# Token mixing in one-unit pieces, with new placement of weight scaling, transposes and the last outputs

## Chip, cores, metric

One core of one Trainium2 chip. The metric is device microseconds of one execution; medians of several runs are given.

## The reference, cut to what matters

```python
# x: (16, 2048, 256) float32; weights 256 x 256; time_mix vectors of 256
x_prev[:, 1:, :] = x[:, :-1, :]
xv = x * time_mix_v + x_prev * (1 - time_mix_v)
xr = x * time_mix_r + x_prev * (1 - time_mix_r)
v = xv @ value_weight
r = xr @ receptance_weight
out = (sigmoid(r) * v) @ output_weight      # the k branch is not used
```

## The kernel before

The 32,768 rows are worked in 64 units of 512 rows, four to a batch. In each unit TensorE transposes x (features on partitions), ScalarE copies the result from PSUM, the memory that TensorE writes to, into `xt` in SBUF, the engines' working memory, and the mix is `xt_prev * c + xt` with `c = 1/tm - 1`, after the weights have been multiplied by `tm`. The mix is one scale per half of the features (`ko`) and one add. Then come two projections (r, v), a sigmoid on ScalarE, the product z on VectorE, the output projection, and a copy and store.

The scale and add of a piece (`piece` is batch, r or v, and a range of columns). POOL, that is GpSimd, takes the second half of the features of some pieces:

```python
def scale(piece, kos=(0, 1)):                  # VectorE, 128 partitions x piece width
    for ko in kos:
        last = nc.vector.tensor_scalar(out=mix[b][:, m, ko, lo:hi], in0=xt[b][:, ko, lo:hi],
                                       scalar1=c_sb[:, m, ko:ko+1], op0=ALU.mult, ...)
    return last

def scale_pool(piece, after):                  # the same for ko = 1 on POOL ...
    op = nc.gpsimd.tensor_scalar(out=mix[b][:, m, 1, lo:hi], in0=xt[b][:, 1, lo:hi], ...)
    tc.add_manual_dep(op.ins, after.ins.name, SYNC, ...)   # ... not before `after` is done

def add(piece):                                # VectorE, both halves at once, both inputs in SBUF
    return nc.vector.tensor_tensor(out=mix[...], in0=mix[...], in1=xt[b][:, :, lo+P:hi+P], op=ALU.add)
```

The loop (cut). After the ramp, as the first eight or so passes are called here, each pass handles one piece of 1024 columns, `held`, and `last` is VectorE's scale of it:

```python
for g in range(NU - 1):
    project(ps_r, g, 0); sigmoid -> s_sb
    for i in todo:
        last = scale(pieces[i], (0,) if i in on_pool else (0, 1))
        if i not in held:
            last = add(pieces[i])
    advance(g + 7)                             # transposes seven units ahead
    project(ps_v, g, 1)
    z_sb = s_sb * ps_v                         # VectorE
    scale_pool(coming[-1], last)               # POOL's half of the next piece
    for i in held: add(pieces[i])
    wrap_slots()                               # once per batch: copy the shifted columns in xt
    output(g - 1, z_prev)
```

At the start two time-mix vectors are loaded with a 4-byte element as the innermost run, and POOL scales the weights.

## Time and profile before

| | before |
|---|---|
| median of the first three runs | 217.93 us (217.86 to 220.3) |
| span of the profiled execution | 217.6 us (this execution took 219.38 us) |
| TensorE / VectorE / ScalarE / POOL busy | 94 / 86 / 84 / 36% |
| first projection, z(0) | 13.39 us, 18.78 us |
| z start to start in the middle | 3.04 to 3.05 us |

A page of the profile gives spans counted from the first instruction; the time of an execution is some 1.8 us longer than its span (219.38 against 217.6). Groups of instructions by shape have these columns: line, engine, operation, output and inputs with their shapes, count, then busy us and mean ns of one, then the idle time of the engine before them and what ended it. Three groups of the kernel before:

```profile
L381 DVE TENSOR_TENSOR z_sb<-s_sb,psum_v 128x1024 bf16<-128x1024 bf16 x63 | 76.9, 1220 | 15.7 <-PE psum_v L235 13.9 <-ACT s_sb L370 1.5
L224 DVE TENSOR_TENSOR mix<-mix,xt 128x2048 bf16<-128x2048 bf16 x60 | 73.8, 1229 | 0.1
L211 POOL TENSOR_SCALAR mix<-xt,c_sb 128x1024 bf16<-128x1024 bf16 x58 | 64.7, 1115 | 107.6 <-DVE mix L200 82.0 <-PE psum_v L235 22.7 <-ACT xt L174 3.0
```

VectorE (DVE) waits 13.9 us in all for the v projection: it has time left. POOL is mostly released by a scale of VectorE (82.0 us of its waiting), and it works beside z in the middle of the run (start, length, what):

```profile
179.80 1.12 POOL L211 TENSOR_SCALAR mix<-xt,c_sb 128x1024 bf16<-128x1024 bf16 x1 [2.03 <-PE psum_v L235]
179.90 1.22 DVE L381 TENSOR_TENSOR z_sb<-s_sb,psum_v 128x1024 bf16<-128x1024 bf16 x1 [0.29 <-PE psum_v L235]
...
181.04 1.22 DVE L224 TENSOR_TENSOR mix<-mix,xt 128x2048 bf16<-128x2048 bf16 x1
```

### The profile page before, as it was taken

To read this page: it belongs to the slowest core of one execution; us is meant where nothing else is said; L and a number is where in the kernel's file an instruction comes from. 1 tells how busy PE (TensorE), PEld (TensorE's weight loads), DVE (VectorE), ACT (ScalarE), POOL (GpSimd) and SP (SyncE) were. 2 spreads that over 40 slices of the span, in tenths; PEclk is the share of its full clock that TensorE was granted. 3 is DMA by queue.
4 is the path that set the end of the run, shared out by engine and by line. 5 is a ranking of instruction groups with operands and counts; after the bars stand their busy time and mean duration, and the time that the engine had idled before them with its cause. 6 is when DMAs were issued, how large, how long until landed. Compare 5 with 4: busy or idle time off the path is not lost.

```text
span 217.6 us, 4124 instructions
## 1 busy us (share of the span) xinstructions
PE 204.7 (94%) x1590; PEld 135.9 (62%) x1590; DVE 186.1 (86%) x236; ACT 183.3 (84%) x196; POOL 78.8 (36%) x103
## 2 busy tenths in 40 slices
PE   8459989999999999999999999999999999999982
PEld 8336755666666666666666666666666666665561
DVE  0297999989898998989889998989998998999932
ACT  2227997999999999999999999999999999987781
POOL 3242423434452445434443345433453234433000
PEclk9957999999999999999999999999999999999999
DMA  5999899999999999999999998989999744335464
GB/s 138 296 219 215 172 164 346 199 270 279 248 286 188 360 166 351 200 289 245 247 285 202 342 172 352 199 295 239 264 270 211 304 194 196 146 143 209 200 270 194
DMA packets 9299, 52.03 MB, mean 239 GB/s; under 512 B 1472, under 2 KB 2368, under 8 KB 3520
## 3 DMA queue, kind: packets, MB, share of 16 engines
q0 software_dynamic: 2304, 16.25, 44.3%
q1 hardware_dynamic: 6144, 35.13, 39.6%
q10 hardware_dynamic: 832, 0.40, 0.6%
q8 instruction: 12, 0.20, 0.3%
q14 instruction: 7, 0.06, 0.1%
HBM read 34.47 MB, written 33.55 MB: 313 GB/s over the span
## 4 chain that ended last, share of the span: by engine, by line
PE 83%; DVE 7%; DMA 4%; issue 3%; ACT 1%; ACTq 0%; DVEq 0%
PE psum_v L235 24%; PE psum_o L245 24%; PE psum_r L235 23%; PE ps_t L169 11%; DMA tm_sb<-in_time_mix_v_dram 4%; DVE mix L224 3%; DVE mix L200 2%; DVE z_sb L381 1%; ACT o_sb L265 0%; DVE z_sb L285 0%; PE psum_v L245 0%; PE psum_r L245 0%; ACT o_sb L296 0%; ACTq L98 0%; ACTq L97 0%
## 5 line engine op out<-in xcount | busy, mean ns | idle before, releaser
L211 POOL TENSOR_SCALAR mix<-xt,c_sb 128x1024 bf16<-128x1024 bf16 (+1 forms) x60 | 66.1, 1101 | 112.8 <-DVE mix L200 84.9
L381 DVE TENSOR_TENSOR z_sb<-s_sb,psum_v 128x1024 bf16<-128x1024 bf16 x63 | 76.9, 1220 | 15.7 <-PE psum_v L235 13.9
L224 DVE TENSOR_TENSOR mix<-mix,xt 128x2048 bf16<-128x2048 bf16 (+2 forms) x69 | 79.9, 1158 | 0.3
L265 ACT COPY o_sb<-psum_o 128x1024 f32<-128x1024 f32 x63 | 64.0, 1016 | 16.0 <-PE psum_o L245 15.9
L235 PEld LDWEIGHTS <-w_bf 128*128 128x128 bf16 x520 | 48.8, 99 | 39.3 <-POOL w_bf L139 3.3
L370 ACT ACTIVATE s_sb<-psum_r 128x1024 bf16<-128x1024 f32 x63 | 65.2, 1034 | 5.4 <-PE psum_r L235 5.4
L235 PE MATMUL psum_r<-mix,w_bf 128*128 128x512 bf16 (+1 forms) x256 | 66.2, 381 | 3.1 <-DVE mix L224 3.1
L235 PE MATMUL psum_v<-mix,w_bf 128*128 128x512 bf16 (+1 forms) x256 | 66.2, 381 | 1.3 <-DVE mix L224 0.8
L245 PE MATMUL psum_o<-wo_bf,z_sb 128*128 128x256 bf16 x504 | 65.3, 273 | 0.2 <-ACT o_sb L265 0.2
L174 ACT COPY xt<-ps_t 128x1024 bf16<-128x1024 bf16 x62 | 63.0, 1030 | 0.0
L245 PEld LDWEIGHTS <-z_sb 128*128 128x128 bf16 x512 | 49.9, 98 | 20.3 <-DVE z_sb L285 1.0
L169 PEld LDWEIGHTS <-x_bf 128*128 128x128 bf16 x496 | 33.3, 100 | 13.8 <-issue 0.5
L169 PE MATMUL ps_t<-ident,x_bf 128*128 128x128 bf16 x496 | 37.9, 222 | 0.0
L200 DVE TENSOR_SCALAR mix<-xt,c_sb 128x1024 bf16<-128x1024 bf16 (+2 forms) x78 | 35.1, 460 | 0.1
L91 POOL DMA_DIRECT2D x_bf<-in_x_dram x16 | 9.3, 583 | 0.0
L128 DVE TENSOR_SCALAR tms<-tm_sb 128x4 f32<-128x4 f32 x1 | 0.2, 171 | 7.8 <-DMA tm_sb<-in_time_mix_v_dram 7.8
L119 PE MATMUL psum_o<-zeros 128*128 128x128 bf16 x34 | 3.8, 313 | 1.0 <-DVE zeros L79 1.0
L119 PEld LDWEIGHTS <-zeros 128*128 128x128 bf16 x34 | 3.5, 150 | 1.0 <-DVE zeros L79 1.0
L174 ACT CAST xt<-psum_o 128x1024 bf16<-128x1024 f32 x1 | 1.0, 1012 | 3.6 <-PE psum_o L169 3.6
L169 PE MATMUL psum_o<-ident_f,x_unit 128*128 128x128 f32 x8 | 1.1, 276 | 2.7 <-DMA x_unit<-in_x_dram 2.7
L139 POOL TENSOR_SCALAR w_bf<-w_f,tms 128x256 bf16<-128x256 f32 x4 | 2.0, 518 | 4.2 <-DVE tms L131 4.1
L322 DVE COPY xt<-xt 128x254 bf16<-128x254 bf16 x15 | 3.3, 220 | 0.0
(38 smaller groups left out, 19.0 us busy)
## 6 DMA issues: line engine op xcount, KB each, us to landing
out_dram<-o_sb SPq DMA_DIRECT2D x30, 1024.0 KB, 5.6
x_bf<-in_x_dram POOLq DMA_DIRECT2D x15, 1024.0 KB, 11.1
out_dram<-o_sb SPq DMA_DIRECT2D x3, 512.0 KB, 2.6
x_unit<-in_x_dram SPq DMA_DIRECT2D x2, 256.0 KB, 3.8
x_unit<-in_x_dram SPq DMA_DIRECT2D x1, 512.0 KB, 7.0
x_bf<-in_x_dram POOLq DMA_DIRECT2D x1, 512.0 KB, 8.5
w_f<-n_receptance_weight_dram SPq DMA_DIRECT2D x1, 256.0 KB, 5.1
w_f<-in_value_weight_dram SPq DMA_DIRECT2D x1, 256.0 KB, 7.2
```

Source lines behind the costliest of these rows:

```text
L91: nc.gpsimd.dma_start(out=x_bf[b][:, lo:hi, :], in_=rows(b)[:, lo:hi, :])
L119: nc.tensor.matmul(out=warm[:, 0, 0:P], lhsT=zeros, rhs=zeros, start=True, stop=True)
L169: nc.tensor.transpose(out=ps[:, ko, jj * P : (jj + 1) * P], in_=src[:, jj, ko * P : (ko + 1) * P], identity=idn,)
L174: nc.scalar.copy(out=xt[b][:, :, c0 : c0 + TU], in_=ps)
L200: last = nc.vector.tensor_scalar(out=mix[b][:, m, ko, lo:hi], in0=xt[b][:, ko, lo:hi], scalar1=c_sb[:, m, ko : ko + 1], scalar2=None, op0= ...
L211: op = nc.gpsimd.tensor_scalar(out=mix[b][:, m, 1, lo:hi], in0=xt[b][:, 1, lo:hi], scalar1=c_sb[:, m, 1:2], scalar2=1.0, op0=ALU.mult, op1 ...
L224: return nc.vector.tensor_tensor(out=mix[b][:, m, :, lo:hi], in0=mix[b][:, m, :, lo:hi], in1=xt[b][:, :, lo + P : hi + P], op=ALU.add,)
L235: nc.tensor.matmul(out=ps[:, mo, :], lhsT=w_bf[:, m, ko, mo * P : (mo + 1) * P], rhs=mix[b][:, m, ko, e * TU + lo : e * TU + hi], start=(k ...
L245: nc.tensor.matmul(out=ps[:, slot, :], lhsT=z[:, ko, jj * P : (jj + 1) * P], rhs=wo_bf[:, ko, :], start=(ko == 0), stop=(ko == KO - 1),)
L265: nc.scalar.copy(out=o_sb[b][:, j0 : j0 + UJ, :], in_=ps)
L370: nc.scalar.activation(out=s_sb, in_=ps_r, func=ACT.Sigmoid)
L381: nc.vector.tensor_tensor(out=z_sb, in0=s_sb, in1=ps_v, op=ALU.mult)
```

## The change

The intent is an earlier start and less work ahead of need. Mixing goes in pieces of one unit (512 columns) shortly before use, transposes run four units ahead, the time-mix vectors come as contiguous rows and are turned by TensorE, the weights are scaled by ScalarE and VectorE (the output weights are cast by their load), ScalarE takes a few scales in the first loop and the last ones, some loads of x are gated behind the first, and the last two outputs go by halves. The core of the diff, with cuts marked:

```diff
-    LOOK = 7
+    LOOK = 4
+    AHEAD = 8
...
+    for m, tm in enumerate([time_mix_r, time_mix_v]):        # contiguous rows, then one transpose
+        nc.scalar.dma_start(out=tm_rows[m*KO:(m+1)*KO, :], in_=tm.rearrange("(ko p) -> ko p", p=P))
     nc.scalar.dma_start(out=x_last, in_=rows(0)[:, J - 1, :])
-    nc.scalar.dma_start(out=tm_sb[:, 0, :], in_=time_mix_r.rearrange("(ko p) -> p ko", p=P))
-    nc.scalar.dma_start(out=tm_sb[:, 1, :], in_=time_mix_v.rearrange("(ko p) -> p ko", p=P))
...
-            nc.gpsimd.tensor_scalar(out=w_bf[:, m, ko, :], in0=w_f32[:, m, ko, :], ...)
+        nc.scalar.activation(out=w_bf[:, 0, ko, :], in_=w_f32[:, 0, ko, :], func=ACT.Copy, scale=...)
...
+        nc.vector.tensor_scalar(out=w_bf[:, 1, ko, :], in0=w_f32[:, 1, ko, :], ...)
...
     for g in range(NU - 1):
+        lead = 2 * g + (4 if g < AHEAD else 5)
+        todo = [pieces(k // 2)[k % 2] for k in range(done, min(lead, 2 * NU))]
+        held = todo[-1:] if lead <= 2 * NU else []
...
+            by_pool = [p for p in pieces(g + 2) if p not in todo or p in held]
...
+        for p in todo:
+            if p[0] in late_copies:
+                wrap_slots()
+            if g > 0:
+                scale(p, [ko for ko in range(KO) if (p, ko) not in elsewhere])
+        for p in todo:
+            if p not in held:
+                last = add(p)
         ps_v = ...; project(ps_v, g, 1)
         z_sb = ...
+        for p in by_pool:
+            scale_pool(p, last)
+        for p in held:
+            add(p)
-        wrap_slots()
```

POOL now has two scales of 512 columns per unit; `last` is now an add, not a scale; and the wrap copy now stands between two scales of VectorE.

More of the change, by code (lines that the diff above doesn't have):

```diff
@@ L47 @@
     NU = B * UB
-    HALF = J * P // 2
-    LOOK = 7
-    SMALL = 2
+    LOOK = 4
     H = UJ // 2
-    START_T = [3, 5, 7, 9]
-    START_MIX = [4, 6, 8, 10, 12]
+    START_T = [1, 3, 5, 6, 7]
+    AHEAD = 8
     WARM = 34
-    WARM2 = 10
+    WARM2 = 12
     consts = ctx.enter_context(tc.tile_pool(name="consts", bufs=1))
@@ L94 @@
     x_unit = consts.tile([P, 2, UJ, D], FP32)
-    tm_sb = consts.tile([P, 2, KO], FP32)
-    w_f32 = consts.tile([P, 3, KO, D], FP32)
+    tm_rows = consts.tile([2 * KO, P], FP32)
+    w_f32 = consts.tile([P, 2, KO, D], FP32)
+    for m, tm in enumerate([time_mix_r, time_mix_v]):
+        nc.scalar.dma_start(
+            out=tm_rows[m * KO : (m + 1) * KO, :], in_=tm.rearrange("(ko p) -> ko p", p=P)
+        )
     nc.scalar.dma_start(out=x_last, in_=rows(0)[:, J - 1, :])
-    nc.scalar.dma_start(out=tm_sb[:, 0, :], in_=time_mix_r.rearrange("(ko p) -> p ko", p=P))
-    nc.scalar.dma_start(out=tm_sb[:, 1, :], in_=time_mix_v.rearrange("(ko p) -> p ko", p=P))
     for h in range(2):
@@ L108, with warm_up @@
     nc.sync.dma_start(out=w_f32[:, 1], in_=value_weight.rearrange("(ko p) n -> p ko n", p=P))
-    nc.sync.dma_start(out=w_f32[:, 2], in_=output_weight.rearrange("(ko p) n -> p ko n", p=P))
     sig0 = consts.tile([P, 1], BF16)
     nc.scalar.activation(out=sig0, in_=zeros[:, 0:1], func=ACT.Sigmoid)
+    w_bf = consts.tile([P, 2, KO, D], BF16)
+    wo_bf = consts.tile([P, KO, D], BF16)
     gate = consts.tile([P, 1], FP32)
     nc.gpsimd.tensor_copy(out=gate, in_=x_last[:, 0:1])
-    load(0, 2 * UJ, J)
-    load(1)
-    warm = ps_o_pool.tile([P, UJ, D], FP32, name="psum_o")
-    for _ in range(WARM):
-        nc.tensor.matmul(out=warm[:, 0, 0:P], lhsT=zeros, rhs=zeros, start=True, stop=True)
+    load(0, 2 * UJ, 3 * UJ)
+    nc.gpsimd.dma_start(out=wo_bf, in_=output_weight.rearrange("(ko p) n -> p ko n", p=P))
+    load(0, 3 * UJ, J)
+    nc.gpsimd.tensor_copy(out=gate, in_=x_unit[:, 1, 0, 0:1])
+    load(1, 3 * UJ, J)
+    load(1, 0, UJ)
+    load(1, UJ, 3 * UJ)
+    load(2)
+    def warm_up(n):
+        ps = ps_t_pool.tile([P, P], FP32, name="ps_t")
+        for _ in range(n):
+            nc.tensor.matmul(out=ps, lhsT=zeros, rhs=zeros, start=True, stop=True)
+    warm_up(WARM)
     def new_xt(b):
@@ L127, with coefficients @@
     c_sb = consts.tile([P, 2, KO], FP32)
-    nc.vector.tensor_scalar(
-        out=tms, in0=tm_sb, scalar1=0.0, scalar2=1e-30, op0=ALU.is_equal, op1=ALU.mult
-    )
-    nc.vector.tensor_tensor(out=tms, in0=tms, in1=tm_sb, op=ALU.add)
-    nc.vector.reciprocal(c_sb, tms)
-    nc.vector.tensor_scalar(out=c_sb, in0=c_sb, scalar1=-1.0, scalar2=None, op0=ALU.add)
-    w_bf = consts.tile([P, 2, KO, D], BF16)
-    wo_bf = consts.tile([P, KO, D], BF16)
-    for m in range(2):
-        for ko in range(KO):
-            nc.gpsimd.tensor_scalar(
-                out=w_bf[:, m, ko, :],
-                in0=w_f32[:, m, ko, :],
-                scalar1=tms[:, m, ko : ko + 1],
-                scalar2=1.0,
-                op0=ALU.mult,
-                op1=ALU.mult,
-            )
-        if m == 0:
-            load(2)
-    nc.gpsimd.tensor_scalar(
-        out=wo_bf, in0=w_f32[:, 2], scalar1=1.0, scalar2=1.0, op0=ALU.mult, op1=ALU.mult
-    )
+    def coefficients():
+        ps = ps_o_pool.tile([P, 2, KO], FP32, name="psum_o")
+        nc.tensor.transpose(
+            out=ps.rearrange("p m k -> p (m k)"), in_=tm_rows, identity=ident_f[: 2 * KO, : 2 * KO]
+        )
+        tm = consts.tile([P, 2, KO], FP32)
+        nc.vector.tensor_copy(out=tm, in_=ps)
+        nc.vector.tensor_scalar(
+            out=tms, in0=tm, scalar1=0.0, scalar2=1e-30, op0=ALU.is_equal, op1=ALU.mult
+        )
+        nc.vector.tensor_tensor(out=tms, in0=tms, in1=tm, op=ALU.add)
+        nc.vector.reciprocal(c_sb, tms)
+        nc.vector.tensor_scalar(out=c_sb, in0=c_sb, scalar1=-1.0, scalar2=None, op0=ALU.add)
+    coefficients()
     def transposes(i):
@@ L178, in first_transposes, with half @@
     def first_transposes():
-        pl = ps_t_pool.tile([P, KO, P], FP32, name="ps_t")
-        for ko in range(KO):
-            nc.tensor.transpose(
-                out=pl[:, ko, 0:P], in_=x_last[:, ko * P : (ko + 1) * P], identity=ident_f
-            )
-        nc.vector.tensor_copy(out=xt[0][:, :, 1:P], in_=pl[:, :, 0 : P - 1])
-        for h, (pool, name) in enumerate([(ps_r_pool, "psum_r"), (ps_v_pool, "psum_v")]):
+        def half(h, pool, name):
             ps = pool.tile([P, KO, TU], FP32, name=name)
@@ L195, in first_transposes @@
             nc.scalar.copy(out=xt[0][:, :, c0 : c0 + H * P], in_=ps[:, :, 0 : H * P])
+        half(0, ps_r_pool, "psum_r")
+        pl = ps_t_pool.tile([P, KO, P], FP32, name="ps_t")
+        for ko in range(KO):
+            nc.tensor.transpose(
+                out=pl[:, ko, 0:P], in_=x_last[:, ko * P : (ko + 1) * P], identity=ident_f
+            )
+        nc.vector.tensor_copy(out=xt[0][:, :, 1:P], in_=pl[:, :, 0 : P - 1])
+        half(1, ps_v_pool, "psum_v")
     def scale(piece, kos=(0, 1)):
@@ L199, in scale @@
         for ko in kos:
-            last = nc.vector.tensor_scalar(
+            nc.vector.tensor_scalar(
                 out=mix[b][:, m, ko, lo:hi],
@@ L206, in scale @@
             )
-        return last
     def scale_pool(piece, after):
@@ L218, in scale_pool @@
         )
-        if after is not None:
-            tc.add_manual_dep(op.ins, after.ins.name, SYNC, reason="one at a time")
+        tc.add_manual_dep(op.ins, after.ins.name, SYNC, reason="one at a time")
     def add(piece):
@@ L281, in last_unit @@
             nc.scalar.activation(out=s_sb[:, :, lo:hi], in_=banks[h], func=ACT.Sigmoid)
-        output(g - 1, z_prev)
         for h, (lo, hi) in enumerate(cols):
@@ L287, in last_unit, with tile_for, pieces, ready @@
             )
-        for h, (pool, name) in enumerate([spare[0], spare[2]]):
+        spare = [(ps_o_pool, "psum_o"), (ps_r_pool, "psum_r"), (ps_v_pool, "psum_v"), (ps_t_pool, "ps_t")]
+        for k, (pool, name) in enumerate(spare):
             ps = pool.tile([P, H, D], FP32, name=name)
+            h = k % 2
             for jj in range(H):
-                out_matmuls(ps, z_sb, h * H + jj, jj)
-            lo = e * UJ + h * H
+                out_matmuls(ps, z_prev if k < 2 else z_sb, h * H + jj, jj)
+            lo = (e - 1) * UJ + k * H
             if h == 0:
+                nc.scalar.copy(out=o_sb[b][:, lo : lo + H, :], in_=ps)
+            else:
                 nc.vector.tensor_copy(out=o_sb[b][:, lo : lo + H, :], in_=ps)
-            else:
-                nc.scalar.copy(out=o_sb[b][:, lo : lo + H, :], in_=ps)
-            store((nc.sync, nc.scalar)[h], b, lo, lo + H)
-    pieces = []
-    for b in range(B):
-        for q in range(2):
-            step = TU if 2 * b + q < SMALL else HALF
-            for lo in range(q * HALF, (q + 1) * HALF, step):
-                pieces += [(b, m, lo, lo + step) for m in range(2)]
-    def needs(piece):
-        b, m, lo, hi = piece
-        if b == 0:
-            return hi // TU
-        return UB * b + min(hi // TU, UB - 1) + 1
-    def tile_for(piece):
-        if piece[0] not in mix:
-            mix[piece[0]] = mixpool.tile([P, 2, KO, J * P], BF16, name="mix")
+            store(nc.scalar if k == 3 else nc.sync, b, lo, lo + H)
+    def tile_for(b):
+        if b not in mix:
+            mix[b] = mixpool.tile([P, 2, KO, J * P], BF16, name="mix")
+    def pieces(g):
+        b, e = divmod(g, UB)
+        tile_for(b)
+        return [(b, m, e * TU, (e + 1) * TU) for m in range(2)]
+    def ready(g):
+        b, e = divmod(g, UB)
+        return tnext > (g if b == 0 else UB * b + min(e + 1, UB - 1))
     def wrap_slots():
@@ L337 @@
     first_transposes()
-    tile_for(pieces[0])
+    tile_for(0)
     for h in range(2):
@@ L342, with scale_act @@
         add(half)
-    scale(pieces[1])
-    add(pieces[1])
-    for _ in range(WARM2):
-        nc.tensor.matmul(out=warm[:, 0, 0:P], lhsT=zeros, rhs=zeros, start=True, stop=True)
-    advance(1)
-    done = 2
-    on_pool = set()
-    def plan(g):
-        upto = START_MIX[g] if g < len(START_MIX) else g + 4 + 2 * SMALL
-        upto = min(upto, len(pieces))
-        for i in range(upto, len(pieces)):
-            assert UB * pieces[i][0] + pieces[i][2] // TU > g + 1, (g, i)
-        return list(range(done, upto))
-    z_prev = None
-    todo = plan(0)
+    for ko in range(KO):
+        nc.scalar.activation(
+            out=w_bf[:, 0, ko, :], in_=w_f32[:, 0, ko, :], func=ACT.Copy, scale=tms[:, 0, ko : ko + 1]
+        )
+    scale(pieces(0)[1])
+    add(pieces(0)[1])
+    for ko in range(KO):
+        nc.vector.tensor_scalar(
+            out=w_bf[:, 1, ko, :],
+            in0=w_f32[:, 1, ko, :],
+            scalar1=tms[:, 1, ko : ko + 1],
+            scalar2=None,
+            op0=ALU.mult,
+        )
+    warm_up(WARM2)
+    advance(1)
+    scale(pieces(1)[0])
+    add(pieces(1)[0])
+    z_prev = None
+    elsewhere = set()
+    done = 3
+    def scale_act(piece, kos):
+        b, m, lo, hi = piece
+        for ko in kos:
+            nc.scalar.activation(
+                out=mix[b][:, m, ko, lo:hi],
+                in_=xt[b][:, ko, lo:hi],
+                func=ACT.Copy,
+                scale=c_sb[:, m, ko : ko + 1],
+            )
+            elsewhere.add((piece, ko))
     for g in range(NU - 1):
-        for i in todo:
-            assert needs(pieces[i]) <= tnext, (g, i, tnext)
-            tile_for(pieces[i])
-        done += len(todo)
+        lead = 2 * g + (4 if g < AHEAD else 5)
+        todo = [pieces(k // 2)[k % 2] for k in range(done, min(lead, 2 * NU))]
+        held = todo[-1:] if lead <= 2 * NU else []
+        done = lead
         ps_r = ps_r_pool.tile([P, KO, TU], FP32, name="psum_r")
@@ L370 @@
         nc.scalar.activation(out=s_sb, in_=ps_r, func=ACT.Sigmoid)
-        last = None
-        held = todo[-1:] if g > 0 else []
-        for i in todo:
-            last = scale(pieces[i], (0,) if i in on_pool else (0, 1))
-            if i not in held:
-                last = add(pieces[i])
-        advance(START_T[g] if g < len(START_T) else g + LOOK)
+        advance(START_T[g] if g < len(START_T) else g + LOOK)
+        if g + LOOK >= NU and g + 2 < NU:
+            scale_act(pieces(g + 2)[1], (0,))
+        by_pool = []
+        if 0 < g < NU - 2 and ready(g + 2):
+            by_pool = [p for p in pieces(g + 2) if p not in todo or p in held]
+        elsewhere.update((p, 1) for p in by_pool)
+        for p in todo:
[6 more added lines that the diff above has]
+                last = add(p)
         ps_v = ps_v_pool.tile([P, KO, TU], FP32, name="psum_v")
         project(ps_v, g, 1)
+        if g == 0:
+            scale_act(todo[0], (0, 1))
+            advance(2)
         z_sb = zpool.tile([P, KO, TU], BF16, name="z_sb")
         nc.vector.tensor_tensor(out=z_sb, in0=s_sb, in1=ps_v, op=ALU.mult)
-        coming = plan(g + 1)
-        for i in coming[-1:]:
-            if needs(pieces[i]) <= tnext:
-                if pieces[i][0] in late_copies:
-                    wrap_slots()
-                tile_for(pieces[i])
-                scale_pool(pieces[i], last)
-                on_pool.add(i)
-        for i in held:
-            add(pieces[i])
-        wrap_slots()
+        for p in by_pool:
+            if p[0] in late_copies:
+                wrap_slots()
+            scale_pool(p, last)
+        for p in held:
+            add(p)
         if z_prev is not None:
@@ L395 @@
         z_prev = z_sb
-        todo = coming
     last_unit(NU - 1)
```

## The prediction

> **What bounds the kernel now.** I read the busy shares first, then the chain that ended last, then the timeline of VectorE (DVE) and GpSimd (POOL). The page's busy line, and the chain: start, length in us, what.
>
> ```profile
> PE 204.7 (94%) x1590; PEld 135.9 (62%) x1590; DVE 186.1 (86%) x236; ACT 183.3 (84%) x196; POOL 78.8 (36%) x103
> ```
>
> ```profile
> 1.66 7.66 DMA tm_sb<-in_time_mix_v_dram
> ...
> 13.39 1.87 PE psum_r L235 x4
> 15.26 1.71 PE ps_t L169 x16
> 16.96 1.72 PE psum_v L235 x4
> ...
> 57.93 0.87 PE psum_o L245 x8
> 60.97 0.87 PE psum_o L245 x8
> ```
>
> TensorE is busy 94%, and in the middle the chain's output groups recur every 3.04 to 3.05 us (57.93 to 60.97). That is its own work for a unit of 512 rows: in the timeline r, v and output take 0.87 each, the eight transposes 0.45, together 3.05. 64 units at 3.05 are 195 us of the 217.6 us span. The rest is the start (first projection at 13.39, held up by two time-mix loads of 1 KB each, the second 7.66 us under way), a ramp to about 37 us, and the end. The first three groups take twice their later time (1.87, 1.71, 1.72 against 0.86, 0.90, 0.86), about 2.7 us lost.
>
> How near the next engine is, the timeline of VectorE shows (start, length, what, in brackets the idle time before):
>
> ```profile
> 176.85 1.22 DVE L381 TENSOR_TENSOR z_sb<-s_sb,psum_v 128x1024 bf16<-128x1024 bf16 x1 [0.29 <-PE psum_v L235]
> 177.99 1.22 DVE L224 TENSOR_TENSOR mix<-mix,xt 128x2048 bf16<-128x2048 bf16 x1
> 179.13 0.48 DVE L200 TENSOR_SCALAR mix<-xt,c_sb 128x1024 bf16<-128x1024 bf16 x1
> 179.90 1.22 DVE L381 TENSOR_TENSOR z_sb<-s_sb,psum_v 128x1024 bf16<-128x1024 bf16 x1 [0.29 <-PE psum_v L235]
> ```
>
> From start to start z takes 1.14 and the add 1.14; the scale ends at 179.61; the idle time is 0.29 us of 3.05. The waits between 37 and 192 us add up to 12.2 us on VectorE in 46 units, 0.27 each. A change that gives VectorE more than this per unit makes it the bound.
>
> The start of the timeline has the two sizes that the change uses, and a collision (POOL is busy from 25.33 to 26.45):
>
> ```profile
> 23.30 0.61 DVE L200 TENSOR_SCALAR mix<-xt,c_sb 128x512 bf16<-128x512 bf16 x2
> 23.94 0.69 DVE L224 TENSOR_TENSOR mix<-mix,xt 128x1024 bf16<-128x1024 bf16 x1
> 25.33 1.12 POOL L211 TENSOR_SCALAR mix<-xt,c_sb 128x1024 bf16<-128x1024 bf16 x1 [2.95 <-ACT xt L174]
> 26.05 0.94 DVE L224 TENSOR_TENSOR mix<-mix,xt 128x1024 bf16<-128x1024 bf16 x1
> ```
>
> The same add takes 0.69 us alone and 0.94 when it starts beside a POOL scale: it ends as if it had begun at 26.30, 0.15 before POOL's recorded end. Four larger adds of the ramp (at 30.48, 35.44, 38.22, 41.04) give 0.14 to 0.15 too.
>
> **What the Trainium skill says.** "SBUF — State Buffer", Who interferes with whom: a VectorE instruction with two SBUF inputs contends with a GpSimd instruction that reads SBUF; whichever starts first has the shared pair for the whole instruction. The trace agrees (0.94 against 0.69). z reads one operand from PSUM, so it should not be held; it took 1.22 beside POOL as elsewhere. "VectorE: DVE Perf Modes", The TRN2 errata: a fixed cost per instruction. It agrees: a scale of 512 columns takes 0.35, of 1024 0.48, so halving pieces nearly doubles the fixed part. "DMA: Bandwidth & Descriptors", Rules for kernel authors: a non-contiguous last dim lowers to one descriptor per element. The slow time-mix loads (4.9 and 7.7 us for 1 KB, against 3.6 us for 128 KB of x) fit. "TensorE: Matmul & The Clock Gate", Part 1: TensorE runs at half rate after an idle window; the doubled groups after an idle wait until 13.39 agree.
>
> **The change, part by part.**
>
> *Time-mix as rows.* Two loads of contiguous rows, one transpose of four columns on TensorE, one copy. Estimate: rows landed by 4.3; the warm-up matmuls end at 4.6 to 4.8; transpose and copy to 5.3; the four small VectorE operations take from 9.42 to 10.39 today, so coefficients at 6.3 in place of 10.39.
>
> *Weights on ScalarE and VectorE, output weights cast by the load, later x loads gated.* POOL is out of the path. The first weights land at 6.75 (1.65+5.1); ScalarE needs about 0.45 each, so they are ready near 8. Half pieces of unit 0: 6.75 to about 8.5. TensorE's order still has the transposes of unit 1 ahead of the first projection; their x landed at 9.1 beside POOL's x loads, which are now smaller or gated, so I take 8.0 plus 1.06. First projection near 9.1: **4.3 us earlier**, after a shorter idle time, so perhaps at full clock.
>
> *Start on VectorE.* From 8.5: the v piece (two scales and add, 1.25) to 9.7; two weight scales to 10.3; the r piece of unit 1, 1.25, to 11.6; z(0) at 11.6 (18.78 today). Then z 1.13 and a held add 0.61 to 13.35, four scales 1.04 and an add 0.61, z(1) at 15.0 (21.43 today). So far 6.4 us gained.
>
> *Steady state: pieces of one unit.* By the instruction order of the built program, VectorE has in each unit scale, scale, add, z, add (adds of 128x1024, scales of 128x512), and POOL two scales of 128x512 where it had one of 128x1024. Start-to-start times from the ramp: scale 0.26 (0.61 for two, the last 0.35), add 0.61, z 1.13. Sum 2x0.26+2x0.61+1.13 = 2.87. The wrap copy, every fourth unit, now stands between two scales and the second waits for it: 0.25 each time, 0.06 per unit. Without collisions 2.93, under 3.05.
>
> But POOL's pair starts only after the first add has completed, and the second add follows z, so they meet. Let the first add start at a. It ends at a+0.69; POOL starts 0.09 to 0.20 later (the gaps in the trace), I take 0.14; POOL's 128x512 scale takes 0.69 (17.54 and 21.70), the next 0.63 after the first; the port is free 0.15 before the recorded end: a+0.69+0.14+0.63+0.69-0.15 = a+2.00. Without POOL the second add would start at a+0.61+1.13 = a+1.74. So it is held 0.26. The loop closes at a+2.00+0.61+0.26+0.26 = a+3.13, with the wrap **3.19 us per unit**, against TensorE's 3.05: VectorE becomes the bound, by 0.14. Lookahead does not help against an engine that lacks time.
>
> *Transposes four ahead.* No work is removed: TensorE's 3.05 per unit stays. Today's last seven loops have no transposes and run at 2.6 to 2.75; now only three do.
>
> *The end.* z(62) started at 208.15 and the span ended 9.45 later. With the last two outputs by halves: z(62) ends 1.2 after its start, v by halves 1.0, then output halves and copies pipelined on both engines, and 3.6 from the last copy to the end as now; I get 8.6, gain 0.8.
>
> *Sum.* z(61) = 15.0+60x3.19 = 206.4; z(62) after a shorter loop (ScalarE and POOL have done its scales) +2.3 = 208.7; +8.6 = 217.3 span, against 217.6. The gain of the start is eaten at 0.14 per unit.
>
> **Rivals.**
> *TensorE stays the bound.* If POOL's pair is some 0.15 us quicker, or an add gets in between, the loop is 3.05. From 9.1, all later TensorE work is 64x2.61+62x0.45 = 195; plus about 1.5 of ramp stalls and 4 from the last matmul to the end: near 209.5. For it: 2.93 without collision fits under 3.05, and someone who moved work so carefully probably looked for this. Against: five adds show the hold.
> *Something between*: a loop of 3.10 to 3.15 gives 212 to 215.
> *Input limits the start.* The x loads by POOL take 8.5 to 11 us; if unit 2's piece is late, up to 2 us of the early gain are lost, hidden wholly or partly if TensorE alone is the bound, added if VectorE is.
> *The clock.* If the first groups again run at half rate, 2.7 us come back on TensorE, but VectorE's chain would hide most of them.
>
> **Range and chances.** The sum says 217.3; each 0.01 in the loop is 0.6 us, and my loop is good to 0.05, so 3 us; TensorE as bound gives 209.5. Six to four between the two, with the ground between filled: 215. Faster by 2% means under 213.6, a loop under 3.13: 0.38. Slower by 2% is over 222.3, a loop over 3.27: 0.04.
>
> **What would show it.** Coefficients near 6.3 and first projection near 9 show the start right. In the middle: z start to start 3.19, TensorE idle about 0.14 per unit waiting for VectorE, VectorE with no idle time and one of its two adds lengthened from 0.69 to about 0.95, show the collision. z start to start 3.05 with VectorE still waiting for psum_v, both adds near 0.69, or POOL done before the second add starts, would show it wrong. A late x_bf in the waits before 17 us would show the input rival.

## The result, and the profile after

The changed kernel takes 226.71 us (226.43 to 226.96, four runs) against 217.94 for the kernel before. The ratio is 1.0375, 95% interval 1.0305 to 1.0445. Ratios here are the mean time of one kernel's fast runs over that of the other's fast runs of the same rounds, so not quite the ratio of the medians. The prediction's estimate was 215, the sum of its working 217.3.

The busy line of the page, and the engines of the chain that ended last:

```profile
PE 211.0 (94%) x1593; PEld 136.4 (61%) x1593; DVE 211.8 (94%) x354; ACT 186.5 (83%) x202; POOL 96.0 (43%) x165
```

```profile
DVE 79%; issue 6%; PE 6%; DMA 3%; POOL 1%; SPq 1%; DVEq 0%; ACT 0%; POOLq 0%
```

TensorE still reads 94% busy, and it is no longer the bound: 79% of the chain is VectorE's. A busy share of 94% for both engines would not have told this; the chain does.

The start went as planned. From the timeline (start, length, what):

```profile
5.84 0.17 DVE L152 TENSOR_SCALAR c_sb<-c_sb 128x4 f32<-128x4 f32 x1
...
9.72 1.03 PE L239 MATMUL psum_r<-mix,w_bf 128*128 128x512 bf16 x4
...
12.23 1.21 DVE L412 TENSOR_TENSOR z_sb<-s_sb,psum_v 128x1024 bf16<-128x1024 bf16 x1
```

Coefficients end at 6.01 us, the first projection starts at 9.72 in place of 13.39 at the pace of the later ones (1.03 for four matmuls, as in the middle), and z(0) at 12.23 in place of 18.78. The clock that the trace shows as granted to TensorE is 1.00 from 9.7 to 15.0 us; before, it was 0.51 from 13.3 to 18.7.

One loop in the middle, the timeline with TensorE's and ScalarE's lines left out:

```profile
102.12 0.68 DVE L228 TENSOR_TENSOR mix<-mix,xt 128x1024 bf16<-128x1024 bf16 x1
...
102.72 1.21 DVE L412 TENSOR_TENSOR z_sb<-s_sb,psum_v 128x1024 bf16<-128x1024 bf16 x1
...
102.97 1.36 POOL L216 TENSOR_SCALAR mix<-xt,c_sb 128x512 bf16<-128x512 bf16 x2 [1.83 <-DVE mix L228]
...
103.86 1.00 DVE L228 TENSOR_TENSOR mix<-mix,xt 128x1024 bf16<-128x1024 bf16 x1
...
104.78 0.60 DVE L206 TENSOR_SCALAR mix<-xt,c_sb 128x512 bf16<-128x512 bf16 x2
...
105.31 0.68 DVE L228 TENSOR_TENSOR mix<-mix,xt 128x1024 bf16<-128x1024 bf16 x1
```

The first add starts at 102.12, the next first add at 105.31: 3.19 us. No idle time stands in brackets on VectorE. The loss is hidden in a length: the second add takes 1.00 where the first takes 0.68. It ends as if it had begun at 104.18, which is 0.15 before the recorded end of POOL's pair (104.33). From z(8) to z(61) z's starts are 3.19 apart in three loops of four and 3.46 in the fourth: 3.26 on average, against 3.05 in a regular loop before. In the fourth the wrap copy stands between two scales, which then start 0.58 apart in place of 0.26:

```profile
111.11 0.34 DVE L206 TENSOR_SCALAR mix<-xt,c_sb 128x512 bf16<-128x512 bf16 x1
111.37 0.21 DVE L324 COPY xt<-xt 128x254 bf16<-128x254 bf16 x1
111.69 0.35 DVE L206 TENSOR_SCALAR mix<-xt,c_sb 128x512 bf16<-128x512 bf16 x1
```

TensorE shows it from its side, with a wait for z that adds up to 4.6 us in 17 waits (before, one of 0.5):

```profile
100.80 1.02 PE L239 MATMUL psum_v<-mix,w_bf 128*128 128x512 bf16 x4 [0.26 <-DVE z_sb L412]
```

In the ramp a second collision appears at two batch boundaries. The wrap copy releases POOL just as VectorE's own scales come:

```profile
20.62 1.64 POOL L216 TENSOR_SCALAR mix<-xt,c_sb 128x512 bf16<-128x512 bf16 x2 [2.74 <-DVE xt L324]
...
20.93 1.48 DVE L206 TENSOR_SCALAR mix<-xt,c_sb 128x512 bf16<-128x512 bf16 x2
```

Two scales that take 0.60 elsewhere take 1.48, and z(2) to z(3) takes 3.88; so does z(6) to z(7). The instructions lengthened here read one tensor each, not two.

Where the 7.3 us between the two spans came from, by the starts of z: z(1) is 5.8 us earlier (15.67 against 21.43); the 60 loops from z(1) to z(61) take 197.7 us against 184.0, 13.7 more; the last loop and the end are 0.6 shorter.

### The profile page after: what moved, and what is told of

It reads as the page before. It is cut to its first block, busy times and chain, and to the rows that moved or that the text cites. A ratio compares the mean times of both kernels' runs of the same rounds, so it can differ in the third digit from the quotient of the medians.

```text
span 224.9 us, 4329 instructions
## 1 busy us (share of the span) xinstructions
PE 211.0 (94%) x1593; PEld 136.4 (61%) x1593; DVE 211.8 (94%) x354; ACT 186.5 (83%) x202; POOL 96.0 (43%) x165
## 4 chain that ended last, share of the span: by engine, by line
DVE 79%; issue 6%; PE 6%; DMA 3%; POOL 1%; SPq 1%; DVEq 0%; ACT 0%; POOLq 0%
DVE mix L228 40%; DVE z_sb L412 29%; DVE mix L206 9%; DMA x_unit<-in_x_dram 3%; PE psum_v L239 2%; POOL mix L216 1%; PE psum_o L249 1%; DVE xt L324 1%; PE psum_r L239 1%; PE ps_t L172 1%; PE psum_o L172 0%; ACT xt L177 0%; PE ps_t L239 0%; DVEq L412 0%; SPq L102 0%
## 5 line engine op out<-in xcount | busy, mean ns | idle before, releaser
L216 POOL TENSOR_SCALAR mix<-xt,c_sb 128x512 bf16<-128x512 bf16 x122 | 83.4, 694 | 112.6 <-DVE mix L228 101.8
L228 DVE TENSOR_TENSOR mix<-mix,xt 128x1024 bf16<-128x1024 bf16 (+1 forms) x129 | 105.2, 817 | 0.3 <-DVE mix L206 0.2
L269 ACT COPY o_sb<-psum_o 128x1024 f32<-128x1024 f32 x62 | 62.8, 1013 | 26.6 <-PE psum_o L249 26.6
L239 PEld LDWEIGHTS <-w_bf 128*128 128x128 bf16 x520 | 49.7, 97 | 45.9 <-issue 7.2
L239 PE MATMUL psum_v<-mix,w_bf 128*128 128x512 bf16 (+1 forms) x256 | 65.1, 376 | 5.9 <-DVE z_sb L412 4.6
L239 PE MATMUL psum_r<-mix,w_bf 128*128 128x512 bf16 (+1 forms) x256 | 65.3, 377 | 0.2
L206 DVE TENSOR_SCALAR mix<-xt,c_sb 128x512 bf16<-128x512 bf16 (+1 forms) x132 | 42.6, 355 | 2.0 <-ACT xt L177 0.5
L90 POOL DMA_DIRECT2D x_bf<-in_x_dram x19 | 11.0, 582 | 0.3 <-issue 0.3
L128 PE MATMUL ps_t<-zeros 128*128 128x128 bf16 x46 | 4.6, 289 | 1.0 <-DVE zeros L78 1.0
L371 ACT ACTIVATE mix<-xt,c_sb 128x512 bf16<-128x512 bf16 x4 | 2.8, 722 | 0.0
```

The source lines that it names most:

```text
L90: nc.gpsimd.dma_start(out=x_bf[b][:, lo:hi, :], in_=rows(b)[:, lo:hi, :])
L128: nc.tensor.matmul(out=ps, lhsT=zeros, rhs=zeros, start=True, stop=True)
L228: return nc.vector.tensor_tensor(out=mix[b][:, m, :, lo:hi], in0=mix[b][:, m, :, lo:hi], in1=xt[b][:, :, lo + P : hi + P], op=ALU.add,)
L239: nc.tensor.matmul(out=ps[:, mo, :], lhsT=w_bf[:, m, ko, mo * P : (mo + 1) * P], rhs=mix[b][:, m, ko, e * TU + lo : e * TU + hi], start=(k ...
L269: nc.scalar.copy(out=o_sb[b][:, j0 : j0 + UJ, :], in_=ps)
```

## The experiments

Eleven runs, each beside the kernel before on the same chip. The changed kernel was not run again; the kernel before had medians of 217.64 to 218.47, so a difference under 1 us says nothing, and those of 3 us or more exceed that spread. For orientation:

| run | median us | ratio to before | z start to start, middle |
|---|---|---|---|
| changed kernel | 226.71 | 1.0375 | 3.26 |
| e1_early: POOL released by the scale | 213.81 | 0.9785 | 3.05 |
| e2_one: POOL has one scale per unit | 223.27 | 1.0245 | 3.20 |
| e3_wrap: wrap copy after the held add | 223.28 | 1.0219 | 3.21 |
| e4_start: start and end of the change alone | 217.46 | 0.9924 | 3.05 |
| e5_look7: transposes seven ahead | 226.11 | 1.0353 | 3.23 |
| e6_early_wrap: both repairs | 212.92 | 0.9744 | 3.05 |
| e7_early_oldtm: e1 with the old time-mix loads | 215.81 | 0.9876 | 3.05 |
| e8_memset: POOL fills in place of a scale (wrong result) | 214.73 | 0.9831 | 3.05 |
| e9_skip2: both repairs, no POOL pair in the third loop | 212.97 | 0.9773 | 3.05 |
| e10_early_again: e1 again | 213.99 | 0.9822 | 3.05 |
| e11_both_again: e6 again | 212.94 | 0.9774 | 3.05 |

**Theory:** POOL's pair, released by an add, meets the held add and holds it. **Rivals:** VectorE simply has too many instructions once the pieces are halved; the wrap copy's place; transposes too late; the new start itself; and that the held add only waits for data, since it reads what POOL's first scale of the pair writes. The last is met by the traces: in the changed kernel that first scale ends at 103.66, before the add starts at 103.86, and e2_one keeps the dependency without the hold.

### e1_early

```diff
-                scale(p, [ko for ko in range(KO) if (p, ko) not in elsewhere])
+                last = scale(p, [ko for ko in range(KO) if (p, ko) not in elsewhere]) or last
...
-                last = add(p)
+                add(p)
```

> POOL's pair of scales is released by VectorE's second scale, not by the first add; nothing else changes. Collision theory: POOL then queues behind the first add for the port, has it some 0.2 us sooner, and the second add is hardly held: the loop closes in about 2.92 us, 3.00 with the wrap copy, so TensorE's 3.05 is the bound again; adds near 0.69, time about 214 (212 to 217). Rival, that VectorE simply has too many instructions with smaller pieces: the loop stays at 3.2 to 3.3, time 225 to 228.

Measured 213.81 us (213.45 to 214.09), 13 us under the changed kernel. Nothing else is different: the same instructions in the same order on every engine. The same stretch of the timeline:

```profile
102.98 0.68 DVE L230 TENSOR_TENSOR mix<-mix,xt 128x1024 bf16<-128x1024 bf16 x1
103.17 1.71 POOL L218 TENSOR_SCALAR mix<-xt,c_sb 128x512 bf16<-128x512 bf16 x2 [0.78 <-DVE mix L207]
...
103.76 1.22 DVE L415 TENSOR_TENSOR z_sb<-s_sb,psum_v 128x1024 bf16<-128x1024 bf16 x1
...
104.90 0.68 DVE L230 TENSOR_TENSOR mix<-mix,xt 128x1024 bf16<-128x1024 bf16 x1
```

POOL's pair now starts 0.19 after the first add has started, and the time it is held falls on POOL: its pair takes 1.71 in place of 1.36 and ends at 104.88, just before the second add, which takes 0.68. Where VectorE sets the pace its loop is 2.89 to 2.90; the wrap loops are 3.20, and in the settled part four loops add up to 12.19 us, which is TensorE's 3.05 each. The rival of too many instructions falls: the same number fits.

### e2_one

```diff
-            by_pool = [p for p in pieces(g + 2) if p not in todo or p in held]
+            by_pool = [p for p in pieces(g + 2) if (p not in todo or p in held) and p[1] == 0]
```

> POOL scales only the r piece; VectorE takes the v piece's second scale, one more instruction of 0.26 us per unit. Collision theory: POOL's single scale ends before the second add starts, the hold of 0.33 goes, the extra 0.26 comes: loop 3.13, 3.20 with the wrap, time 222 to 225, a little under the changed kernel. Rival, too many VectorE instructions: the 0.26 is added in full, loop 3.45 or more, time 238 to 243.

Measured 223.27 (222.93 to 225.97). The adds by shape, first of the changed kernel, then of this run:

```profile
L228 DVE TENSOR_TENSOR mix<-mix,xt 128x1024 bf16<-128x1024 bf16 x127 | 104.3, 823 | 0.3 <-DVE mix L206 0.2
L228 DVE TENSOR_TENSOR mix<-mix,xt 128x1024 bf16<-128x1024 bf16 x127 | 86.4, 681 | 0.2
```

With more work on VectorE the kernel is faster, by 3.4 us in the median (by the ratios, which take in one run of 225.97, by 2.8). All adds are at 0.68 (0.82 on average in the changed kernel), regular loops are 3.12: the hold of 0.33 is gone and a scale of 0.26 came. This one is as the theory said, to 0.01 in the loop.

### e3_wrap

```diff
         for p in held:
             add(p)
+        wrap_slots()
```

> The wrap copy is issued after the held add of the unit in which its source is ready, not between two scales that wait for it. If the copy's place costs: every fourth loop 3.33 in place of 3.46, 15 times 0.14, so about 2 us less, 224 to 225. If its place does not matter: 226.7.

Measured 223.28, 3.4 us under the changed kernel, more than the 2 expected. Four loops now take 3.33, 3.13, 3.18 and 3.19, together 12.83 against 13.03: 0.20 each time, 2.6 us in the thirteen times from z(8) to z(61). Another 0.6 comes from the ramp, where z(6) to z(7) takes 3.30 in place of 3.88. The wrap copy's place costs, because the second scale waits for it; but it is the smaller part.

### e4_start

The changed kernel's start and its end by halves, joined to the loop, the pieces and the lookahead of the kernel before (too long to show as a diff; it is the changed text up to the definition of the pieces and the old text from there).

> The changed kernel's start (time-mix rows, weights on ScalarE and VectorE, gated loads) and end by halves, with the pieces, POOL scale and transposes seven ahead of the kernel before. Collision theory, that all the loss is in the steady state: middle at 3.05 per unit, first projection near 9.7 in place of 13.4, time 212 to 216. Rival, that the early start only moves the wait (VectorE bound in the ramp, input late): 216 to 219.

Measured 217.46 (215.58 to 217.98), ratio 0.9924: the theory's 212 to 216 was too low, and the rival's 216 to 219 holds. The timeline says why:

```profile
11.40 0.62 PE L174 MATMUL ps_t<-ident,x_bf 128*128 128x128 bf16 x8 [1.72 <-DMA x_bf<-in_x_dram]
...
13.58 1.04 PE L174 MATMUL ps_t<-ident,x_bf 128*128 128x128 bf16 x8 [1.56 <-DMA x_bf<-in_x_dram]
...
14.41 1.92 PE L244 MATMUL psum_v<-mix,w_bf 128*128 128x512 bf16 x4
...
16.43 1.22 DVE L402 TENSOR_TENSOR z_sb<-s_sb,psum_v 128x1024 bf16<-128x1024 bf16 x1 [3.59 <-PE psum_v L244]
```

The old loop wants units 2 and 3 transposed before the first v projection. Their x has not landed, TensorE waits 1.72 and 1.56 us, and then runs the first groups at half speed again (1.92; granted clock 0.50 from 14.4 to 18.0). The first projection starts at 8.66, earlier than the 9.7 expected; but z(0) is at 16.43, and z(4) at 33.35 against 34.31: 1.0 us is left. So the early start is worth little with the old order of the first transposes. The changed kernel transposes only unit 1 before its first v projection. The run swaps loop, pieces and lookahead together, so what the smaller pieces add to this is not shown.

### e5_look7

```diff
-    LOOK = 4
+    LOOK = 7
-    START_T = [1, 3, 5, 6, 7]
+    START_T = [1, 3, 5, 7, 9, 11]
```

(The condition for ScalarE's help in the last loops was kept at four.)

> The changed kernel with transposes seven units ahead, as in the kernel before. Collision theory: VectorE and POOL set the pace, so lookahead of the transposes does not matter: 225.5 to 228. Rival, that four ahead is too short and its copies arrive late: 222 or less.

Measured 226.11. The loops in the middle are a little shorter (3.23), since only every second wrap copy still makes a loop of 3.51, and the ramp with its extra transposes is longer (z(8) at 42.33 against 40.74). The lookahead of the transposes is not the cause: the regular loop stays at 3.19.

### e6_early_wrap

The edits of e1_early and e3_wrap together.

> Both repairs: POOL released by the second scale, and the wrap copy after the held add. If the first repair already leaves TensorE as the bound in the middle, the second only helps where VectorE is the bound, in the ramp (the loop of 3.88 at z(6) becomes about 3.3): 213.0 to 213.6, against 213.8. If the wrap still costs in each fourth loop: about 211.

Measured 212.92 (212.52 to 212.93), the fastest so far and just under the 213.0 to 213.6 of the first expectation. The engines of the chain that ended last:

```profile
PE 86%; DMA 5%; ACT 3%; DVE 1%; issue 1%; POOL 1%; ACTq 0%
```

TensorE is the bound again. z(6) to z(7) is 3.05 in place of 3.88 (3.3 was expected), and 38 of the 53 loops from z(8) to z(61) are 3.04 to 3.05.

### e7_early_oldtm

```diff
-        nc.scalar.dma_start(out=tm_rows[m*KO:(m+1)*KO, :], in_=tm.rearrange("(ko p) -> ko p", p=P))
-    nc.scalar.dma_start(out=x_last, ...)
+    nc.scalar.dma_start(out=x_last, ...)
+    nc.scalar.dma_start(out=tm_sb[:, 0, :], in_=time_mix_r.rearrange("(ko p) -> p ko", p=P))
+    nc.scalar.dma_start(out=tm_sb[:, 1, :], in_=time_mix_v.rearrange("(ko p) -> p ko", p=P))
...                                              # and no transpose of tm_rows
```

> The first repair with the time-mix loads of the kernel before (4-byte elements, x_last first). It measures what the rows are worth when the middle is bound by TensorE: coefficients near 10.4 in place of 6.0. If the chain of VectorE carries the delay to the end: 4 us more, about 217.5. If the input or the ramp hides it: 214 to 215.

Measured 215.81 (214.71 to 216.47), between the two expectations. Against e1_early (by the ratios to before) it is 0.9% or 2 us slower, against e10_early_again 0.5%; the intervals overlap (0.9817 to 0.9935, 0.9739 to 0.983, 0.9788 to 0.9856), so the size is rough. The coefficients end at 9.26 us, not near 10.4 as expected, against 5.85 in e1_early. z(0) is at 15.13 against 12.03; of these 3.1 us, the span keeps 2.4 (214.7 against 212.3), since the next loops are shorter (3.39 and 3.19 in place of 3.70 and 3.49).

### e8_memset

```diff
         for p in by_pool:
-            scale_pool(p, last)
+            if p[1] == 0:
+                scale_pool(p, last)
+            else:                                   # wrong result on purpose
+                nc.gpsimd.memset(mix[p[0]][:, 1, 1, p[2]:p[3]], 0.0)
+                nc.gpsimd.memset(scratch, 0.0)
```

> Wrong results on purpose: in the changed kernel POOL's second scale is replaced by two fills that read nothing and together last at least as long, so POOL is as busy beside the second add as before. Theory that POOL's reading holds the add: second add back to 0.69, loop near 2.9, TensorE bound, 212 to 215. Rival, that any work of POOL in that place, or the add's wait on POOL, holds it: adds near 1.0, time 225 to 229.

The result is wrong. Measured 214.73. The groups by shape:

```profile
L228 DVE TENSOR_TENSOR mix<-mix,xt 128x1024 bf16<-128x1024 bf16 x127 | 86.6, 683 | 0.4 <-DVE mix L206 0.2
L216 POOL TENSOR_SCALAR mix<-xt,c_sb 128x512 bf16<-128x512 bf16 x61 | 42.6, 699 | 85.6 <-DVE mix L228 71.2 <-ACT xt L177 8.4 <-DVE xt L324 6.0
L421 POOL MEMSET scratch<- 128x512 f32 x61 | 31.9, 523 | 0.0
L420 POOL MEMSET mix<- 128x512 bf16 x61 | 31.9, 523 | 0.0
```

POOL is still released by the add, and by the profile is busy longer than before (0.69 and two fills of 0.52; spans on POOL are rough, but the fills' starts, 0.46 apart, agree), right beside the second add: one is at 102.60 to 103.29 while the fills run from 102.16 to 103.15. Yet that add takes 0.69. So it is not POOL's being busy that holds the add. What the fills lack is the reading of SBUF, which is what the theory names; that they are also another operation is a difference that no run separates.

### e9_skip2, e10_early_again, e11_both_again

e9 is e6 without POOL's pair in the third loop (`g != 2` in the condition); the other two repeat e1 and e6 on one chip.

> Both repairs, and no POOL pair in the third loop, where the wrap copy releases it just as VectorE's scales come (z interval 3.88, two scales 1.48). VectorE takes the two scales, 0.52. If the collision there costs more than that: interval about 3.1 then 3.6, 0.3 us less than both repairs alone; if the ramp is set by something else: the same within 0.3.

> The first repair again, unchanged, beside both repairs on one chip: 213.8 again, or the ratio 0.979.

> Both repairs again, unchanged: if the wrap copy's place is worth something where TensorE is the bound in the middle, 0.5 to 1 us under the first repair alone on the same chip; otherwise the same.

Measured 212.97, 213.99 and 212.94. The third loop of e9 is 3.76 in place of 3.88 (3.1 was expected) and the next 3.27 in place of 3.13, so e9 gives nothing. Its trace shows why:

```profile
20.86 1.14 DVE L207 TENSOR_SCALAR mix<-xt,c_sb 128x512 bf16<-128x512 bf16 x4
```

With POOL idle each scale takes 0.35, where beside POOL's pair each takes about 0.75; so the hold is real, but four scales without it last nearly as long as two with it.

The wrap copy's place is worth 1.0 us on one chip (213.99 against 212.94). By the traces this is earned in the ramp: z(1) to z(8) takes 23.78 in place of 24.68, while z(8) to z(61) takes 160.2 against 160.4. Where TensorE is the bound the place costs next to nothing. The kernel with both repairs beats the kernel before by 2.3% (0.9774, 0.9741 to 0.9807) in this call (unclear at 2%) and 2.6% in the earlier one (faster), and the changed kernel by about 6%.

## Why the prediction was wrong, point by point

The estimate was 215, and the median 226.7. The way from one to the other is 2.3 us for the weighting of rivals, 6.9 for z(61), 0.7 for the end, and 1.8 for a span used as a time.

- **The step that failed** is "z(61) = 15.0+60x3.19 = 206.4", one loop length for all sixty loops. z(61) started at 213.35. Of the 6.9 us, 0.7 are a late z(1), 2.7 the seven loops to z(8), and 3.5 the 53 loops after it. The mechanism behind it was right; its cost per loop was put too low. The prediction had the sixty loops eat the gain of the start (191.4 us against 184.0); they took 197.7, and so ate more than twice what the start had gained (13.7 us against z(1)'s 5.8).
- **The bound.** That TensorE's 3.05 us bound the kernel before, and that VectorE had little to spare, is right: e1_early brings 3.05 back. The 0.27 us per unit is misread: the 12.2 us are 46 waits in 51 loops, so 0.24 per loop. Nothing later rests on it.
- **The start.** Coefficients near 6.3 (6.01 measured), first projection near 9.1 (9.72), z(0) at 11.6 (12.23), z(1) at 15.0 (15.67): right, all but the coefficients a little late. x of unit 1 was taken to land at 8.0; its transposes waited for it until 8.82.
- **The mechanism of the steady state.** POOL's pair meets the second add and VectorE becomes the bound: right, shown by e1_early, e2_one and e8_memset.
- **The size of the loop.** In the regular loop the prediction put POOL's start 0.14 after the add and the second scale 0.63 after the first; measured are 0.17 and a pair of 1.36 (0.69 each, hardly overlapping), so 3.19 in place of 3.13. The wrap cost 0.27 in place of 0.25 every fourth loop. Together the step "3.19 us per unit" was 3.26: from z(8) to z(61) 172.6 us against 53 x 3.19 = 169.1.
- **The ramp.** z(1) to z(8) took 25.1 us against 7 x 3.19 = 22.3. Two of these loops took 3.88, where the wrap copy releases POOL against VectorE's scales, and the eighth 4.06, where it takes on a third piece. Neither was counted. The prediction named only instructions with two SBUF inputs as held; these scales have one tensor input and were lengthened too.
- **The end.** The last loop was 0.3 longer than the 2.3 put down, and the stretch after z(62) 0.4 longer than the 8.6. (The last loops of the kernel before ran at 2.48 to 2.77, not quite "2.6 to 2.75".) With these the 217.3 becomes the 224.9 us of the profile.
- **Span and time.** The 217.3 was a span and was used as a time; an execution takes 1.8 us more (226.70 for a span of 224.9). The same working as a time would have been 219.1.
- **The choice.** "Six to four between the two" gave weight to the rival in which TensorE stays the bound, on a guess about the author's care, against five measured holds. That took 2.3 us off the working's own sum, which as a time was still 8 us short.
- **The lookahead** was rightly given no effect in either direction (e5_look7), and the late input, put down as a rival, shows in e4_start, though not as the cause of the slowdown.

Not settled: what a loop of 3.48 us in the changed kernel (at 142 us), and the like in the other runs, is due to; such loops appear once or twice per run, and in the changed kernel VectorE waits 0.2 us there between a scale and the add after it. Nor why the profiled execution of the kernel before took 1.4 us more than its median.

## What to carry to other kernels

When work is split over two engines that share a port to memory, count not only how much each does but what runs beside what: releasing GpSimd by an earlier instruction moved the same work to where nobody waited for it, and was worth 13 of 227 us. In these traces an engine held at the shared port shows no idle time, only a longer instruction, so compare the length of one and the same instruction between two kernels before believing busy shares. An earlier start pays only if the next loops don't ask for data that lands later.

## What the Trainium skill lacked or had wrong

- "SBUF — State Buffer", Who interferes with whom, agrees with the runs on three points: the hold itself (an add of 0.68 took 1.00), that a GpSimd instruction which only writes does not hold it (0.69 beside two fills), and that the first to start wins (in e1_early POOL was held instead, pair 1.71 in place of 1.36). The same page (section "SBUF: two separate sides") has the lock last "for the whole instruction". To judge by its length, the held add runs from 0.15 us before the recorded end of POOL's pair; whether the lock ends early or the record runs past it, the runs can't tell.
- "Perfetto Trace Analysis", Per-instruction lifecycle, says that waits fall outside the recorded window. For semaphores this agrees (z's wait of 0.29 us stands before its 1.22, not in it); a wait for the shared port falls inside it, as a longer instruction (0.32 us here), and no page says so.
- No page gives the cost of releasing GpSimd from VectorE: its scale started 0.09 to 0.21 us after the end of the releasing instruction. Nor that two GpSimd scales of 512 columns in a row hardly overlap (1.36 for two of 0.69), where a later fill overlapped by 0.06.
